# MLP activations at another offset in SBUF, and products that read and write their columns in short runs from two halves

## The chip, the cores and the metric

The kernel runs on one core of one Trainium2 chip. The metric is the device time of one execution in microseconds (us). TensorE (PE in the profile) does the matrix products, VectorE (DVE) and ScalarE (ACT) the element-wise work, GpSimd (POOL) some of it too; weights come from HBM by DMAs that the queue of SyncE (SP) issues.

## The reference, cut to what matters

A trunk of two layers over 512 tokens with 1024 channels, in float32. Each layer is a mixer and a gated MLP, both with a residual add. The MLP, which the change touches in both layers:

```python
def conv_ffn(x, w_up, conv_w, conv_b, w_down):
    hdn = causal_dwconv(x @ w_up, conv_w, conv_b)
    return (jax.nn.silu(hdn[..., :D_FF]) * hdn[..., D_FF:]) @ w_down
...
h = rmsnorm(x, norm_ffn[i]); x = x + conv_ffn(h, f_w_up[i], ...)      # D_FF = 2816, kernel of 3 taps
```

The mixer of layer 0 (an mLSTM) has an output gate, `h * jax.nn.sigmoid(o)` with `o` a slice of `x @ w_in`, 1024 columns wide; its product is the second place that the change touches.

## The kernel before, in words

Everything is held transposed: channels on the 128 partitions, the 512 tokens along the free axis. A float32 operand is split into a high and a low float32r part, and a product is three matrix products (`mm3`, L160 to L163): stationary high part times moving high part (L161), high times low (L162), low times high (L163). In all the products that the change touches the weights (`wh`, `wl`) are the stationary operand, 128 rows by 128 columns, and the activations are the moving one, 128 rows by 512 columns. Each of the three is one instruction that loads the weights (LDWEIGHTS) and one that streams the columns (MATMUL) and adds them to one bank of PSUM.

`proj` (L404) multiplies one unit of weights (8 blocks of 128x128) by the normed input `xh`, `xl`: 8 x 3 = 24 products into one bank. It makes the queries and keys (`qk_conv`), the output gates (`o_block`, L432, eight blocks), the up-projections of both MLPs (`ffn`, L593) and the input of the convolution module (`glu`).

`ffn` runs in two parts. Up: 22 times (`j`), two calls of `proj` into two banks `pa` and `pb`, then on VectorE and ScalarE the row factor of the norm, three taps, silu and the gate, which leave `yh[:, j, :]` and `yl[:, j, :]`, the two parts of the hidden activations. Down: for each of 8 output blocks `m`, 22 x 3 = 66 products of the down-weights by `yh` and `yl` into one bank. In the last MLP the last block (`m` = 7) is made in two halves of 256 columns, 132 products in all. So the first MLP has 44 x 24 = 1056 products up and 528 down, the second 1056 up, 462 down and those 132 halves, and the eight output gates are 192 products.

The units of weights come in a fixed order (`seq`). `next_unit` has up to four units in flight by DMA and splits two ahead, ScalarE the high part (L149), VectorE the low one (L150). The order of the instructions on each engine is laid down when the program is built, by a scheduler.

Where tiles lie in a partition of SBUF follows from the order and sizes of the pools. In the built program, byte addresses modulo 256 are: `xh` and `xl` 64, all eight pairs; each 128-column block of `wh` and `wl` 64; `yh` and `yl` 0 for every `j`, in both MLPs (`fp`, the pool of the MLP, starts with them). In the two projections after the mixers (`out_proj`, L576 to L580) the moving operand lies elsewhere: `gh` and `gl` of layer 0 start at 0, 32, 64, 96, 128, 160, 192 and 224, one pair of blocks each, `zht` and `zlt` of layer 1 at 128.

Of the kernel before, what the change touches and what calls it, by code (L numbers as in the profile page):

```python
# [9 lines left out]
F32 = mybir.dt.float32  # L10
# [4 lines left out]
P = 128  # L15
T = 512
D = 1024
KD = D // P
# [6 lines left out]
EPS = 1e-6  # L25
QSCALE = 128.0 ** -0.5
NEG = -1.0e30
NPH = 4                    # token phases of the convolution on the tensor engine
NTAU = T // NPH
NJ = (CK + 2 * NPH - 3) // NPH  # L30
GR = 68                    # rows: input gates at 0, running maximum at 32, forget gates at 64

# column offsets in the packed per-channel parameter array
_COLS = {}
_off = 0
for _n, _w in [("norm_mix", 16), ("norm_ffn", 16), ("norm_final", 8), ("mconv_w", 32),
# [9 lines left out]
def hybrid_trunk(ctx, tc, x_in, par_in, tph_in, wg_in, wv_in, wqk_in, wo_in, mout_in, cin_in,  # L46
# [20 lines left out]
    def small():  # L67
        return psms.tile([P, T], F32, tag="ms", name=nm("ms"))

# [1 line left out]
    par = const.tile([P, NPAR], F32, name="par")  # L71
    nc.scalar.dma_start(out=par[:, :16], in_=par_in[:, :16])

# [18 lines left out]
    G.memset(mhalf, -0.5)  # L92

    def warm(n, after=None):
        """Products that nobody reads, to keep the clock of the tensor engine up over a wait."""
        ps = bank()
        for _ in range(n):
            with tc.issue_after(after.ins) if after is not None else nullcontext():
                after = PE.matmul(ps[:, :P], ones, ones, start=True, stop=True)  # L99

# [1 line left out]
    seq = []  # L102
    for h in range(2):
        for u in range(4):
# [57 lines left out]
        PE.matmul(ps, lh, rl, start=False, stop=False)  # L162
        PE.matmul(ps, ll, rh, start=False, stop=stop)  # L163

# [1 line left out]
    xh = [None] * KD  # L166
    xl = [None] * KD

# [27 lines left out]
        return t[:, c].rearrange("p (a b) -> p a b", b=P)  # L196

    def to_rows(src, c, tag):
        """Values along the free axis, equal on all partitions -> [128 tokens, blocks]."""
        nb = (c.stop - c.start) // P  # L200
        dg = work.tile([P, T], F32, tag="tmp", name=nm("dg"), bufs=4)
        V.tensor_tensor(out=blocks(dg, c), in0=src,
                        in1=ident[:].unsqueeze(1).to_broadcast([P, nb, P]), op=ALU.mult)
        r4 = work.tile([P, NTB], F32, tag=tag, name=nm(tag))
        V.tensor_reduce(out=r4[:, :nb], in_=blocks(dg, c), op=ALU.add, axis=mybir.AxisListType.X)
        return r4

    def from_rows(r4, nb, pb):
        """[128 tokens, blocks] -> the values along the free axis on all partitions (PSUM)."""
        hl = work.tile([P, 2, NTB], F32R, tag="hl", name=nm("hl"))  # L210
        V.tensor_copy(hl[:, 0, :nb], r4[:, :nb])
        V.tensor_tensor(out=hl[:, 1, :nb], in0=r4[:, :nb], in1=hl[:, 0, :nb], op=ALU.subtract)
        for i in range(2):
            dg = work.tile([P, NTB, P], F32R, tag="tmp", name=nm("dgr"), bufs=4)
            v = V.tensor_tensor(out=dg[:, :nb], in0=ident[:].unsqueeze(1).to_broadcast([P, nb, P]),
                            in1=hl[:, i, :nb].bitcast(F32).unsqueeze(2).to_broadcast([P, nb, P]),
                            op=ALU.mult)
            p = PE.matmul(pb, onesr, dg[:, :nb].rearrange("p a b -> p (a b)"), start=i == 0, stop=i == 1)  # L218
        return v, p

    def col_mean(ps, t, c, w):
        """Sum over the partitions of t times the constant in w, on all partitions."""
        h = work.tile([P, T], F32R, tag="tmp", name=nm("ch"), bufs=4)
        l = work.tile([P, T], F32R, tag="tmp", name=nm("cl"), bufs=4)
        A.copy(h[:, c], t[:, c])
        V.tensor_tensor(out=l[:, c], in0=t[:, c], in1=h[:, c], op=ALU.subtract)
        PE.matmul(ps, w, h[:, c], start=True, stop=False)
        PE.matmul(ps, w, l[:, c], start=False, stop=True)
# [4 lines left out]
        return o4  # L233

    def row_sums(ps, t, c, w, start, stop):
        """Adds the sums over the partitions of t, times w, to ps: [128 tokens, 2 * blocks]."""
        nb = (c.stop - c.start) // P
        for b in range(nb):
            s = slice(c.start + b * P, c.start + (b + 1) * P)
            PE.matmul(ps[:, 2 * b : 2 * b + 2], t[:, s], w[:, :2], start=start and b == 0,  # L240
                      stop=stop and b == nb - 1)

    def norm_rows(nrm, c):
        """1 / rms of the tokens in c, [128 tokens, blocks]."""
        n = c.stop - c.start
        ps = small()
        col_mean(ps[:, :n], nrm.acc, c, invdr)
        r4 = to_rows(ps[:, :n].rearrange("p (a b) -> p a b", b=P), c, "ms4")
        V.tensor_scalar(out=r4[:, : n // P], in0=r4[:, : n // P], scalar1=EPS, scalar2=None,
                        op0=ALU.add)  # L250
        return rsqrt4(r4, n // P, "rs4")

    # the row factors of a norm are worked out between the first products of the next stage
    hooks = []

    def run_hook():
# [15 lines left out]

    rs = {}

    # ================= layer 0: mLSTM =================
    warm(9)
    nrm = Norm()
    first = wraw.tile([P, 1024], F32, tag="wr", name="wr0")
# [76 lines left out]

    pv = v_pair(0)

    # gates, channel-major: input gates on partitions 0-3, forget gates on 32-35
    wgh, wgl = next_unit()
    pg = small()  # L360
    for k in range(KD):
# [39 lines left out]
                                       in1=t[:, s:], op0=ALU.mult, op1=ALU.add)  # L401
        return v

    def proj(units, ps):  # L404
        wh, wl = units
        for k in range(KD):
            c = slice(k * P, (k + 1) * P)
            mm3(ps, wh[:, c], wl[:, c], xh[k], xl[k], k == 0, k == KD - 1)
            if k == 5:
                run_hook()  # L410

# [19 lines left out]

    def o_block(m, ahead=2):  # L432
        ps = bank()
        proj(next_unit(ahead), ps)
        sig[m] = mp.tile([P, T], F32, tag="sig", name=nm("sig"), bufs=4)
        V.tensor_tensor(out=sig[m], in0=ps, in1=rs["b"], op=ALU.mult)
        A.activation(sig[m], sig[m], AF.Sigmoid)
# [1 line left out]
    T0 = [0, 128, 256, 256]  # L439

    def att_decay(h):
        """exp of the decay from s to t less the running maximum; s on partitions, t free."""
        plf, pm = small(), small()
        for p, i in ((plf, h), (pm, NH + h)):
            PE.matmul(p, sel[:, i, :], sth, start=True, stop=False)
# [82 lines left out]
    q = qk(0)  # L528
# [60 lines left out]
    out_proj(gh, gl_, None, lambda m: ("norm_ffn", m))  # L589
    mctx.close()  # L590

    # ================= gated MLP with a depthwise convolution =================
    def ffn(l, g=None, last=False):  # L593
        fctx = ExitStack()
        fp = fctx.enter_context(tc.tile_pool(name=nm("ffn"), bufs=1))
        yh = fp.tile([P, NF, T], F32R, name=nm("yh"))
        yl = fp.tile([P, NF, T], F32R, name=nm("yl"))
        for j in range(NF):
            pa, pb = bank(), bank()
            proj(next_unit(), pa)  # L600
            proj(next_unit(), pb)
            ta = fp.tile([P, T], F32, tag="ta", name=nm("ta"), bufs=2)
            tb = fp.tile([P, T], F32, tag="tb", name=nm("tb"), bufs=2)
            both = ((pa, ta, l * 44 + j), (pb, tb, l * 44 + NF + j))
# [85 lines left out]

    ffn(0, lambda m: ("norm_mix", 8 + m))

    # ================= layer 1: convolution module =================
    cctx = ExitStack()
    cp = cctx.enter_context(tc.tile_pool(name="conv", bufs=1))
    DVE_CH, POOL_CH, PE_CH = (0, 2, 4), (1,), (3, 5, 6, 7)
# [4 lines left out]
    pdvr = cp.tile([P, P], F32R, name="pdvr")  # L701
    A.copy(pdvr, p128)
    cacc = {c: cp.tile([P, T], F32, name=f"cacc{c}") for c in range(8)}
    # 1 where the partition lies in the block of NPH partitions
    tph = cp.tile([P, 8 * 4 * NJ * NPH], F32, name="tph")
    nc.sync.dma_start(out=tph, in_=tph_in)
    msk4 = cp.tile([P, P // NPH, 1], F32, name="msk4")
# [74 lines left out]
                o = 32 * (2 * hf + g)  # L782
                (nc.scalar if g == 0 else nc.sync).dma_start(out=back[o : o + 32], in_=co[:, g])

    # taps for the vector engine and GpSimd, handed out between the products
    vtaps, gtaps = [], []

    def background(nv, ng):
# [9 lines left out]
    FIRST, LAST = PE_CH[0], PE_CH[-1]  # L798

    def shift():  # L800
        """The mean of one block of channels, by which all values are shifted before their sums."""
        d[FIRST] = cp.tile([P, T], F32, name=f"d{FIRST}")
        A.activation(d[FIRST].rearrange("p (t q) -> p t q", q=NPH),
                     cacc[FIRST].rearrange("p (q t) -> p t q", q=NPH), AF.Identity,
                     bias=pcol("dw_b", FIRST))
        pk = small()
        col_mean(pk, d[FIRST], slice(0, T), pdvr)
        A.copy(kb, pk)
        V.tensor_tensor(out=d[FIRST], in0=d[FIRST], in1=kb, op=ALU.subtract)
        G.tensor_copy(s1, d[FIRST])  # L810
        A.activation(s2, d[FIRST], AF.Square)
# [49 lines left out]
    sq4 = stats(4, V)  # L861
    sq7 = stats(LAST, None)

    # layer norm over channels
    pr1, pr2, pmu = small(), small(), bank()
    for i, (t1, t2) in enumerate(((s1, s2), (d[LAST], sq7))):
        row_sums(pr1, t1, slice(0, T), invd, i == 0, i == 1)
# [34 lines left out]
def _layout(inputs):  # L902
    f = {k: np.asarray(v) for k, v in inputs.items()}

    def ch(a):  # [..., C] -> [128, ... * C/128], channel c = m * 128 + p
        a = a.reshape(a.shape[:-1] + (-1, P))
        return np.moveaxis(a, -1, 0).reshape(P, -1)

    def taps(w):  # [K, C] -> [128, C/128 * K]
        k, c = w.shape  # L910
        return w.reshape(k, c // P, P).transpose(2, 1, 0).reshape(P, -1)

    def cols(w, n=P):  # [K, N] -> [N/n, 128, K/128 * n]
        k, c = w.shape
        return w.reshape(k // P, P, c // n, n).transpose(2, 1, 0, 3).reshape(c // n, P, -1)

    # gate biases: input gates on partitions 0-3, forget gates on 32-35
    bg = np.zeros((P, 1), np.float32)
    bg[0:4, 0], bg[32:36, 0] = f["m_b_gates"][0][:4], f["m_b_gates"][0][4:]
    # taps by token phase: dph[c * NPH + p, m, g, j, q] = w[K - 1 - (NPH * j + q - p), m * 128 + g * 32 + c]  # L920
    dw = f["c_dw_w"][0].reshape(CK, KD, 4, P // 4)
    dph = np.zeros((P // NPH, NPH, KD, 4, NJ, NPH), np.float32)
    for p in range(NPH):
# [50 lines left out]
```

## Time and profile before

| what | value |
|---|---|
| two timed runs | 1192.22 and 1192.62 us, median 1192.42 |
| profiled execution, first to last instruction (span) | 1191.0 us |
| that lies outside the span, median less span | 1.4 us |
| PE busy | 1134.3 us, 95% of the span |
| PE in the chain that ended last | 84% |

The profiled execution is known by its span alone, so it stands beside the median with what lies around the span. Matrix products are pipelined: the time shown for one (0.39 us) is longer than the distance from its start to the start of the next, and that distance, called pace here, is what a stage of back-to-back products costs. It is read from the starts in a timeline: last start less first start, divided by the products between.

### The profile page before, as it was taken

The numbers are of one execution on the slowest core, as the hardware profiler recorded it, in microseconds if no ns is written. First come the engines' busy times: TensorE is split into PE (matmuls) and PEld (weight loads), VectorE is DVE, ScalarE is ACT, GpSimd is POOL, SyncE is SP. The second block draws the span as 40 slices with busy tenths as digits, with TensorE's granted clock in tenths as the row PEclk, the third lists the DMA queues.
The fourth block names the chain that finished last, engine by engine and source line by source line (L and its number), as shares of the span: only waits on it lengthen the run. The fifth ranks groups of instructions, "written<-read, shape, count | busy, mean of one in ns | idle before, by whom it ended". The sixth has DMA issues, their size and how long they took to land.

```text
span 1191.0 us, 13476 instructions
## 1 busy us (share of the span) xinstructions
PE 1134.3 (95%) x5226; PEld 939.7 (79%) x5226; DVE 788.6 (66%) x1022; ACT 510.8 (43%) x713; POOL 174.8 (15%) x126
## 2 busy tenths in 40 slices
PE   9999999999999999999998757699999999999996
PEld 7788888888888888888887647588888888888886
DVE  6788875487777775332479999874877777752222
ACT  6556774354444443222244522363544444432221
POOL 4000001100000000000267857021000000000002
PEclk9999999999999999999998879699999999999998
DMA  6222123223232323233332112022232323233322
GB/s 247 89 89 71 54 74 103 90 89 106 89 106 89 105 86 92 90 97 98 110 105 62 62 44 67 14 88 89 92 103 90 106 89 106 84 98 89 93 62 71
DMA packets 36369, 106.85 MB, mean 90 GB/s; under 512 B 4049, under 2 KB 10321, under 8 KB 36305
## 3 DMA queue, kind: packets, MB, share of 16 engines
q1 hardware_dynamic: 31728, 103.25, 27.2%
q10 hardware_dynamic: 4576, 2.74, 0.8%
q8 instruction: 41, 0.67, 0.2%
q14 instruction: 24, 0.19, 0.0%
HBM read 101.78 MB, written 2.10 MB: 87 GB/s over the span
## 4 chain that ended last, share of the span: by engine, by line
PE 84%; DVE 13%; issue 1%; ACT 1%; DMA 1%; POOL 0%; ACTq 0%; POOLq 0%; SPq 0%; DVEq 0%
PE mm L161 25%; PE mm L162 25%; PE mm L163 25%; DVE cacc L744 8%; PE mm L580 2%; PE mm L577 2%; PE mm L576 2%; DVE wl L150 2%; PE ms L240 1%; PE mm L99 0%; DMA xall<-in_dram 0%; PE ms L218 0%; DVE u L722 0%; DVE se L453 0%; DVE s L826 0%
## 5 line engine op out<-in xcount | busy, mean ns | idle before, releaser
L163 PE MATMUL mm<-xh,wl 128*128 128x512 f32 x960 | 375.6, 391 | 3.3 <-DVE wl L150 3.3
L161 PE MATMUL mm<-xh,wh 128*128 128x512 f32 x960 | 375.6, 392 | 0.0
L162 PE MATMUL mm<-xl,wh 128*128 128x512 f32 x960 | 375.4, 391 | 0.0
L150 DVE TENSOR_TENSOR wl<-wr,wh 128x1024 fp32r<-128x1024 f32 (+1 forms) x192 | 236.5, 1235 | 165.5 <-ACT wh L149 163.3
L149 ACT CAST wh<-wr 128x1024 fp32r<-128x1024 f32 (+1 forms) x192 | 197.4, 1030 | 296.1 <-PE mm L162 243.6
L163 PEld LDWEIGHTS mm<-xh,wl 128*128 128x128 f32 x960 | 181.4, 189 | 41.9 <-DVE wl L150 3.7
L162 PEld LDWEIGHTS mm<-xl,wh 128*128 128x128 f32 x960 | 181.4, 189 | 37.9
L161 PEld LDWEIGHTS mm<-xh,wh 128*128 128x128 f32 x960 | 181.5, 189 | 37.2
L193 POOL TENSOR_TENSOR acc<-acc,sq 128x512 f32<-128x512 f32 x30 | 43.3, 1444 | 746.7 <-ACT sq L191 746.2
L161 PE MATMUL mm<-yh,wh 128*128 128x512 f32 (+1 forms) x374 | 142.3, 380 | 0.0
L162 PE MATMUL mm<-yl,wh 128*128 128x512 f32 (+1 forms) x374 | 142.3, 380 | 0.0
L163 PE MATMUL mm<-yh,wl 128*128 128x512 f32 (+1 forms) x374 | 142.2, 380 | 0.0
L606 DVE TENSOR_TENSOR mm<-mm,rsb 128x512 f32<-128x512 f32 x88 | 60.8, 695 | 76.0 <-PE mm L163 73.1
L744 DVE SCALAR_TENSOR_TENSOR cacc<-u,par,cacc 128x501 f32<-128x501 f32 (+27 forms) x80 | 102.1, 1321 | 0.1
L161 PEld LDWEIGHTS mm<-yh,wh 128*128 128x128 f32 x374 | 70.0, 187 | 15.5
L162 PEld LDWEIGHTS mm<-yl,wh 128*128 128x128 f32 x374 | 70.0, 187 | 15.3
L163 PEld LDWEIGHTS mm<-yh,wl 128*128 128x128 f32 x374 | 70.0, 187 | 15.2
L616 ACT CAST yh<-ta 128x512 fp32r<-128x512 f32 x44 | 27.3, 620 | 104.6 <-DVE ta L615 104.6
L611 DVE SCALAR_TENSOR_TENSOR ta<-mm,par,ta 128x511 f32<-128x511 f32 x88 | 65.6, 745 | 1.3
L611 DVE SCALAR_TENSOR_TENSOR tb<-mm,par,tb 128x511 f32<-128x511 f32 x88 | 65.5, 746 | 1.4
L614 ACT ACTIVATE ta<-ta 128x512 f32<-128x512 f32 x44 | 27.8, 632 | 79.4 <-DVE ta L611 79.4
L741 POOL TENSOR_TENSOR cacc<-cacc,cprod 128x511 f32<-128x511 f32 (+29 forms) x30 | 49.5, 1651 | 24.1 <-ACT cprod L739 22.4
(237 smaller groups left out, 1200.5 us busy)
## 6 DMA issues: line engine op xcount, KB each, us to landing
wr<-in_dram SPq DMA_DIRECT2D x175, 512.0 KB, 3.5
wr<-in_dram SPq DMA_DIRECT2D x16, 384.0 KB, 3.1
xall<-in_dram SPq DMA_DIRECT2D x8, 256.0 KB, 6.4
us<-u ACTq DMA_DIRECT2D x16, 64.0 KB, 2.1
out_dram<-xall SPq DMA_DIRECT2D x2, 384.0 KB, 3.5
tph<-in_dram SPq DMA_DIRECT2D x1, 576.0 KB, 4.5
wr<-in_dram SPq DMA_DIRECT2D x2, 256.0 KB, 3.9
cacc<-co ACTq DMA_DIRECT2D x8, 64.0 KB, 2.4
```

The costliest lines, as they stand in the source:

```text
L149: st["last"] = A.copy(hi[:, :n], r[:, :n])
L150: V.tensor_tensor(out=lo[:, :n], in0=r[:, :n], in1=hi[:, :n], op=ALU.subtract)
L161: PE.matmul(ps, lh, rh, start=start, stop=False)
L162: PE.matmul(ps, lh, rl, start=False, stop=False)
L163: PE.matmul(ps, ll, rh, start=False, stop=stop)
L193: e.tensor_tensor(out=nrm.acc[:, c], in0=nrm.acc[:, c], in1=sq[:, c], op=ALU.add)
L606: V.tensor_tensor(out=ps, in0=ps, in1=rs["b"], op=ALU.mult)
L611: V.scalar_tensor_tensor(out=t[:, s:], in0=ps[:, : T - s], scalar=pcol("fconv_w", m * 3 + 2 - s), in1=t[:, s:], op0=ALU.mult, op1=ALU.add)
L614: A.activation(ta, ta, AF.Silu)
L616: A.copy(yh[:, j, :], ta)
L741: G.tensor_tensor(out=a[:, s:], in0=a[:, s:], in1=p[:, s:], op=ALU.add)
L744: V.scalar_tensor_tensor(out=cacc[j][:, s:], in0=u[:, : T - s], scalar=dw(j, CK - 1 - s), in1=cacc[j][:, s:], op0=ALU.mult, op1=ALU.add)
```

## The change

There are two edits. (1) Each MLP takes a small unused tile at the head of its pool, 16 floats (64 bytes) in the first MLP and 8 floats (32 bytes) in the second. All tiles of that pool move up by as much: `yh` and `yl` lie at 64 modulo 256 in the first MLP and at 32 in the second, and `ta` and `tb` move with them. (2) `proj` takes a run length `e`. With `e` above 0 the moving operand and the PSUM output are seen as two halves of 256 columns that are cut in runs of `e` columns, and the product walks them as run 0 of the first half, run 0 of the second, run 1 of the first, and so on. Input and output are walked alike, so each column lands where it did. The output gates use `e` = 4 (128 runs of 16 bytes), the up-projection of the first MLP `e` = 32 (16 runs of 128 bytes), and all other calls `e` = 0, which is the plain operand of before. Comments go too.

```diff
-    def proj(units, ps):
+    def runs(t, e):
+
+        return t.rearrange("p (h c e) -> p c h e", h=2, e=e) if e else t
+
+    def proj(units, ps, e=0):
         wh, wl = units
         for k in range(KD):
             c = slice(k * P, (k + 1) * P)
-            mm3(ps, wh[:, c], wl[:, c], xh[k], xl[k], k == 0, k == KD - 1)
+            mm3(runs(ps, e), wh[:, c], wl[:, c], runs(xh[k], e), runs(xl[k], e), k == 0, k == KD - 1)
...
     def o_block(m, ahead=2):
         ps = bank()
-        proj(next_unit(ahead), ps)
+        proj(next_unit(ahead), ps, 4)
...
         fp = fctx.enter_context(tc.tile_pool(name=nm("ffn"), bufs=1))
+        fp.tile([P, 16 >> l], F32, name=nm("pad"))
         yh = fp.tile([P, NF, T], F32R, name=nm("yh"))
         yl = fp.tile([P, NF, T], F32R, name=nm("yl"))
         for j in range(NF):
             pa, pb = bank(), bank()
-            proj(next_unit(), pa)
-            proj(next_unit(), pb)
+            proj(next_unit(), pa, 32 if l == 0 else 0)
+            proj(next_unit(), pb, 32 if l == 0 else 0)
```

No engine's instructions change their order; the shapes of the touched products do. On PE, where the second key block ends and the first output gate begins (`mm_640` and `mm_688` are their banks), before:

```order
L162 MATMUL mm_640<-xl_17_162,wh_605 128x512
L163 MATMUL mm_640<-xh_16_161,wl_606 128x512
L161 MATMUL mm_688<-xh_2_110,wh_643 128x512
L162 MATMUL mm_688<-xl_3_111,wh_643 128x512
L163 MATMUL mm_688<-xh_2_110,wl_644 128x512
L161 MATMUL mm_688<-xh_4_116,wh_643 128x512
```

and now:

```order
L162 MATMUL mm_640<-xl_17_162,wh_605 128x512
L163 MATMUL mm_640<-xh_16_161,wl_606 128x512
L161 MATMUL mm_688<-xh_2_110,wh_643 128x64x2x4
L162 MATMUL mm_688<-xl_3_111,wh_643 128x64x2x4
L163 MATMUL mm_688<-xh_2_110,wl_644 128x64x2x4
L161 MATMUL mm_688<-xh_4_116,wh_643 128x64x2x4
```

The 192 products of the gates are walked as 64 x 2 runs of 4 columns. On PE, where the first MLP goes from the first block of its up-projection to the next (`mm_2059`, then `mm_2160`), now:

```order
L161 MATMUL mm_2059<-xh_256_2044,wh_2062 128x8x2x32
L162 MATMUL mm_2059<-xl_257_2045,wh_2062 128x8x2x32
L163 MATMUL mm_2059<-xh_256_2044,wl_2063 128x8x2x32
L161 MATMUL mm_2160<-xh_229_1803,wh_2106 128x8x2x32
L162 MATMUL mm_2160<-xl_230_1804,wh_2106 128x8x2x32
```

Its 1056 products are 8 x 2 runs of 32 columns, in the places where 128x512 stood.

## Rows read from the trace of the kernel before

**Rows 1.** The page: busy times, the clock in 40 slices, the chain by engine.

```profile
PE 1134.3 (95%) x5226; PEld 939.7 (79%) x5226; DVE 788.6 (66%) x1022; ACT 510.8 (43%) x713; POOL 174.8 (15%) x126
...
PEclk9999999999999999999998879699999999999998
...
PE 84%; DVE 13%; issue 1%; ACT 1%; DMA 1%; POOL 0%; ACTq 0%; POOLq 0%; SPq 0%; DVEq 0%
```

**Rows 2.** Busy time by stretch: start:end, length, busy us (instructions), granted clock, DMA share.

```profile
core 0: us, PE busy (x) PEld busy (x) DVE busy (x) ACT busy (x) POOL busy (x), PEclk, DMA share, GB/s
58.00:175.00 117.00, 116.07 (x591) 98.51 (x590) 97.56 (x185) 80.95 (x150) 4.04 (x4) 1.00 0.22 75
...
220.40:460.70 240.30, 240.30 (x1061) 198.93 (x1060) 175.63 (x226) 106.99 (x134) 1.02 (x1) 1.00 0.30 96
460.70:583.90 123.20, 123.20 (x529) 98.75 (x529) 39.90 (x43) 33.58 (x40) 7.77 (x6) 1.00 0.31 93
...
815.30:1055.60 240.30, 240.30 (x1061) 198.95 (x1060) 175.69 (x226) 105.69 (x133) 1.02 (x1) 1.00 0.30 96
1055.60:1172.00 116.40, 116.40 (x539) 94.96 (x538) 33.20 (x35) 32.60 (x39) 7.71 (x6) 1.00 0.26 75
```

**Rows 3.** Timeline, PE, first up-projection: start, time shown; 45 products apart.

```profile
329.74 0.39 PE L162 MATMUL mm<-xl,wh 128*128 128x512 f32 x1
...
339.94 0.39 PE L162 MATMUL mm<-xl,wh 128*128 128x512 f32 x1
```

**Rows 4.** Timeline, PE, first down-projection; 27 products apart.

```profile
479.66 0.39 PE L161 MATMUL mm<-yh,wh 128*128 128x512 f32 x1
...
485.96 0.39 PE L161 MATMUL mm<-yh,wh 128*128 128x512 f32 x1
```

**Rows 5.** Timeline, PE, output gates of layer 0; 12 products apart.

```profile
69.77 0.39 PE L161 MATMUL mm<-xh,wh 128*128 128x512 f32 x1
...
72.49 0.39 PE L161 MATMUL mm<-xh,wh 128*128 128x512 f32 x1
```

**Rows 6.** Chain that ended last, projections after the mixers: start, us, eight products.

```profile
190.79 1.87 PE mm L580 x8
...
797.15 1.83 PE mm L580 x8
```

**Rows 7.** Timeline, PE, projection after the mLSTM: moving operands at mixed offsets.

```profile
192.72 0.39 PE L577 MATMUL mm<-gl,wh 128*128 128x512 f32 x1
192.96 0.40 PE L576 MATMUL mm<-gh,wh 128*128 128x512 f32 x1
```

**Rows 8.** Timeline, PE, last block in halves of 256 columns; 18 products apart.

```profile
1174.95 0.28 PE L161 MATMUL mm<-yh,wh 128*128 128x256 f32 x1
...
1176.99 0.28 PE L161 MATMUL mm<-yh,wh 128*128 128x256 f32 x1
```

**Rows 9.** Groups of the first up-projection: busy us, mean ns, idle before.

```profile
L162 PEld LDWEIGHTS mm<-xl,wh 128*128 128x128 f32 x352 | 66.1, 188 | 13.9
...
L150 DVE TENSOR_TENSOR wl<-wr,wh 128x1024 fp32r<-128x1024 f32 x44 | 53.9, 1224 | 11.6 <-ACT wh L149 10.7
...
L606 DVE TENSOR_TENSOR mm<-mm,rsb 128x512 f32<-128x512 f32 x43 | 29.7, 695 | 36.1 <-PE mm L163 34.6 <-ACT rsb L269 1.5
```

## The prediction, made before the changed kernel ran

> **What bounds the kernel now.** I read the page first: PE is busy 95% of the span and 84% of the chain that ended last [rows 1]. Then the stretches: both MLPs are PE from end to end, 240.3 of 240.3 us and 123.2 of 123.2 us, at the full granted clock, while VectorE is busy 175.6 of 240.3 us at most; the stretch of the mLSTM with the output gates is PE too, 116.1 of 117.0 us [rows 2]. Next to nobody is waited for there, so what sets their length is the pace of the products, and the timeline gives it. Up, at 64 modulo 256 for moving operand and weights: (339.94 - 329.74) / 45 = 226.7 ns [rows 3]. The output gates, with the same operands: 2.72 / 12 = 226.7 ns [rows 5]. Down, with `yh` at 0 and the weights at 64: 6.30 / 27 = 233.3 ns [rows 4]. Shape, clock and order of instructions are the same in both, and VectorE is less busy in the slower one (39.9 of 123.2 us) [rows 2], so neither the clock nor another engine's traffic makes the difference; what is left is where the operands lie. Pace times count gives the stages back: 1056 x 226.7 = 239.4 us of the 240.3, 528 x 233.3 = 123.2 us. The projections after the mixers bear it out: 1.87 / 8 = 234 ns with the moving operand at mixed offsets, 1.83 / 8 = 229 ns with it at 128 [rows 6]. [...]
>
> **First MLP down (528 products).** `yh` and `yl` come to 64, the offset at which `xh` is read against the same weights. I take the pace of the up-projection: 528 x (226.7 - 233.3) = -3.5 us. The bounds: 226.7 is the lowest pace in any row, so -3.5 on one side; on the other the longest distance in the mixed stage, 192.96 - 192.72 = 240 ns [rows 7], which is 528 x 6.7 = +3.5 us.
>
> [...]
>
> **Second MLP down (462 products, 132 halves).** At 32 the operand lies halfway between two offsets that have rows (0 and 64). No row shows 32 alone; the stage with all offsets mixed has 234 ns. Bounds: 226.7 and 240 ns, which are -3.1 and +3.1 us. I take the middle of the two neighbours, 230 ns: 462 x (230 - 233.3) = -1.5 us. [...]
>
> **Up-projection and gates in runs (1056 and 192 products).** [...] The nearest row is that of the halves: two products of 256 columns cost 226.6 ns together, no more than one of 512 and less than the one of the same operands, 233.3, so beginning anew in the middle cost nothing there. I take 0 for both. [...]
>
> [...]
>
> **The sum.** -3.5 - 1.5 + 0 + 0 = -5.0 us. The profiled span of 1191.0 us becomes 1186.0, and with the 1.4 us outside it that the median of 1192.42 shows, 1187.4 us. Everything behind these stages starts earlier by what they save: the convolution module in between waits for VectorE's taps, which follow the products of its own input, so it moves as a whole.
>
> **Rivals.** [...] (b) *Each break costs.* The product pauses when it jumps to the other half, in reading SBUF or in writing PSUM. A product makes 15 jumps at `e` = 32 and 127 at `e` = 4: 1056 x 15 + 192 x 127 = 40,224. From 5.0 us / 40,224 = 0.12 ns per jump it eats the gain. [...] For it: nothing has shown such a stream at speed. Against it: the halves [rows 8]. (c) *The offset does nothing and the runs neither*: the difference between up and down comes from something that I don't see, and the time stays at 1192.4 us.
>
> **How the numbers follow.** Forecast 0.33, with its own range 1184 to 1192 us (the bounds of the second MLP, and some of the first). (a) 0.27, 1171 to 1183. (b) 0.32: half of that under 24 us, half above, since four cycles per jump are as conceivable as one. (c) 0.08. The range leaves out the far end of (a) and the far half of (b): 1175 to 1216 us. A measurement of this kernel can tell about 2% from no change, 23.8 us: slower by that is the far half of (b), 0.15; faster by that would be below 1168.6 us, past even the whole of (a), 0.02; within, 0.83.
>
> **What would show it.** In the changed profile: the first down-projection at 226.7 ns per product, 119.7 us long instead of 123.2 (right), or still 233.3 (the address is not the cause). The second: its pace tells what 32 is worth. [...] I am wrong if the up-projection of the first MLP differs from the second by more than 3 us.

## The result, and the profile of the changed kernel

Two timed runs took 1204.07 and 1205.78 us, median 1204.92, against 1192.42 before: a ratio of 1.0104 with the interval [1.0075, 1.0133]. The kernel became about 12.5 us slower, where 5 us less was forecast. The profiled span grew from 1191.0 to 1202.4 us, by 11.4 us.

The page of the changed kernel, its busy times and the granted clock, answers to [rows 1]; the third line is the group of all products of `xh` and `wl` that `proj` makes, the plain ones included (busy us, mean ns, idle before):

```profile
PE 1144.4 (95%) x5226; PEld 940.9 (78%) x5226; DVE 791.3 (66%) x1022; ACT 510.7 (42%) x713; POOL 174.8 (15%) x126
...
PEclk9999999999999999999999969699999999999998
...
L163 PE MATMUL mm<-xh,wl 128*128 128x512 f32 x960 | 380.5, 396 | 3.3 <-DVE wl L150 3.3
```

The same group before:

```profile
L163 PE MATMUL mm<-xh,wl 128*128 128x512 f32 x960 | 375.6, 391 | 3.3 <-DVE wl L150 3.3
```

PE makes the same 5226 products in 10.1 us more, at the same clock (mean granted 0.976, before 0.974), and stands idle for 3.3 us in all ahead of the 960 products of that group, as before. So nothing new is waited for: the products themselves take longer. Which ones, the stretches tell (start:end, length, busy us per engine, clock; answers to [rows 2]):

```profile
core 0: us, PE busy (x) PEld busy (x) DVE busy (x) ACT busy (x) POOL busy (x), PEclk, DMA share, GB/s
224.40:475.20 250.80, 250.80 (x1062) 200.43 (x1061) 177.30 (x226) 105.82 (x134) 1.02 (x1) 1.00 0.29 92
475.20:594.80 119.60, 119.60 (x530) 98.99 (x529) 39.94 (x43) 33.71 (x40) 7.87 (x6) 1.00 0.32 95
826.20:1066.60 240.40, 240.40 (x1062) 199.07 (x1061) 175.67 (x226) 105.75 (x133) 1.02 (x1) 1.00 0.30 96
```

Compared with [rows 2] the first up-projection starts 4.0 us later (224.40 for 220.40) and lasts 250.8 us for 240.3, the first down-projection 119.6 for 123.2, the convolution module 231.4 for 231.4, the second up-projection 240.4 for 240.3, and what follows to the end 135.8 for 135.4: 4.0 + 10.5 - 3.6 + 0.1 + 0.4 = 11.4 us, the whole of it. In the stage that grew, the clock is 1.00, VectorE is busy 177 of 251 us, and the loading of weights 200 of 251.

The paces, from the timeline of PE of the changed kernel. In order of time: gates, first up, first down, second down, halves; they answer to [rows 5], [rows 3], [rows 4] and [rows 8], and the second down-projection to [rows 4] too:

```profile
69.16 0.41 PE L161 MATMUL mm<-xh,wh 128*128 128x512 f32 x1
...
72.17 0.42 PE L161 MATMUL mm<-xh,wh 128*128 128x512 f32 x1
...
332.84 0.40 PE L162 MATMUL mm<-xl,wh 128*128 128x512 f32 x1
...
343.49 0.40 PE L162 MATMUL mm<-xl,wh 128*128 128x512 f32 x1
...
489.61 0.39 PE L161 MATMUL mm<-yh,wh 128*128 128x512 f32 x1
...
495.73 0.39 PE L161 MATMUL mm<-yh,wh 128*128 128x512 f32 x1
...
1070.19 0.40 PE L161 MATMUL mm<-yh,wh 128*128 128x512 f32 x1
...
1076.49 0.40 PE L161 MATMUL mm<-yh,wh 128*128 128x512 f32 x1
...
1186.37 0.28 PE L161 MATMUL mm<-yh,wh 128*128 128x256 f32 x1
...
1188.50 0.28 PE L161 MATMUL mm<-yh,wh 128*128 128x256 f32 x1
```

The gates: 3.01 us / 12 products = 250.8 ns, where it was 226.7. First up: 10.65 / 45 = 236.7, where it was 226.7. First down: 6.12 / 27 = 226.7, where it was 233.3. Second down: 6.30 / 27 = 233.3, unchanged. Halves: 2.13 / 18 = 118.3, where it was 113.3. Note that the time shown beside a start (0.39 or 0.40 us) says next to nothing of this: only the distance of the starts does.

So the runs cost 1056 x 10 = 10.6 us and 192 x 24 = 4.6 us, the new address brought 528 x 6.6 = 3.5 us in the first MLP, and in the second it cost 132 x 5 = 0.7 us in the halves: 12.4 us in sum, beside 12.5 between the medians and 11.4 between the two spans. Per jump the two costs are 10 / 15 = 0.67 ns at runs of 32 columns and 24 / 127 = 0.19 ns at runs of 4: no fixed price per jump.

### The profile page after: what moved, and what is told of

The parts are those of the page before. It is cut to its first block, busy times and chain, and to the rows that moved or that the text cites. A ratio compares the mean times of both kernels' runs of the same rounds, so it can differ in the third digit from the quotient of the medians.

```text
span 1202.4 us, 13474 instructions
## 1 busy us (share of the span) xinstructions
PE 1144.4 (95%) x5226; PEld 940.9 (78%) x5226; DVE 791.3 (66%) x1022; ACT 510.7 (42%) x713; POOL 174.8 (15%) x126
## 4 chain that ended last, share of the span: by engine, by line
PE 84%; DVE 13%; issue 1%; ACT 1%; DMA 1%; POOL 0%; ACTq 0%; POOLq 0%; SPq 0%; DVEq 0%
PE mm L162 25%; PE mm L161 25%; PE mm L163 25%; DVE cacc L749 8%; PE mm L584 2%; PE mm L581 2%; PE mm L580 2%; DVE wl L150 2%; PE ms L240 1%; DMA xall<-in_dram 0%; PE ms L218 0%; DVE u L727 0%; DVE se L457 0%; DVE s L831 0%; PE mm L521 0%
## 5 line engine op out<-in xcount | busy, mean ns | idle before, releaser
L163 PE MATMUL mm<-xh,wl 128*128 128x512 f32 x960 | 380.5, 396 | 3.3 <-DVE wl L150 3.3
L161 PE MATMUL mm<-xh,wh 128*128 128x512 f32 x960 | 380.8, 397 | 0.0
L162 PE MATMUL mm<-xl,wh 128*128 128x512 f32 x960 | 380.5, 396 | 0.0
```

The lines of the kernel that those rows point to most:

```text
L161: PE.matmul(ps, lh, rh, start=start, stop=False)
```

## The experiments

Below, a pace is the mean distance between the starts of successive products of one stage, waits left out; the timelines show two starts each, so a pace worked out from them can differ by some tenths of a ns from that of the whole stage. "Offset" is the byte address of the moving operand less that of the weights, modulo 256. Where one time is given, the kernel was run once, beside kernels before at 1192.8 to 1194.7 us; what is read from it rests on paces, which repeat between runs (runs of 32 take 236.7 ns in the changed kernel and in `sides`, a plain product at the offset 192 takes 233.3 in the kernel before and in `weights_shift`), and not on the total. Several kernels add other columns than the reference does, or leave out part of the sums; the expectations say which.

Two theories were in the field for most of it. Theory M: the stream of columns meets the stream that loads the next weights in one part of SBUF, and the offset and the runs change how often. Theory S: the stream of columns stands in its own way, by the order in which it comes back to the same bytes modulo 256.

### Each edit alone

```diff
# pads_only
+        if (16, 8)[l]:
+            fp.tile([P, (16, 8)[l]], F32, name=nm("pad"))
# runs_only
+    def proj(units, ps, rd=0, wr=0):
+            mm3(runs(ps, wr), wh[:, c], wl[:, c], runs(xh[k], rd), runs(xl[k], rd), k == 0, k == KD - 1)
...
+        proj(next_unit(ahead), ps, 4, 4)
...
+            proj(next_unit(), pa, *((32, 32), (0, 0))[l])
```

> Edit 1 alone: yh and yl at 64 modulo 256 in the first MLP, at 32 in the second, no runs. If the two edits add up (theory: each stage's pace depends on its own operands alone), the first down-projection runs at 226.7 ns per product, the second at 233.3, its halves at 118 to 120 ns, both up-projections and the gates at 226.7: 1192.4 - 3.5 + 0.8 = 1189.7 us. Rival: part of the gain in the first down-projection came from the runs ahead of it, and the time is 1192 or more.

> Edit 2 alone. If the edits add up: gates at 250 ns per product, first up-projection at 236.6, both down-projections at 233.3 as before; span 1191.0 + 192 x 23.4 + 1056 x 9.9 = 1191.0 + 4.5 + 10.5 = 1206 us. Rival: the new place of ta and tb or of yh had a part in the slower up-projection, which then runs below 236 ns here.

The pads alone took 1189.77 us (1189.28 to 1191.80) beside 1193.73, a ratio of 0.9973 [0.9964, 0.9983]: 3.2 us less by the ratio (the medians are 4.0 apart). First down 226.7 ns, second down 233.3, halves 118.2, gates and up 226.7 to 227. The runs alone took 1207.45 us: gates 250.3, first up 236.7, both down-projections 233.3. The paces of the two edits appear unchanged in the changed kernel, so they don't act on each other, and the runs hold the whole loss.

### Reading or writing in runs

```diff
# sides: proj(units, ps, rd, wr); queries and keys written in runs, gates read in runs
+        proj(next_unit(), ps, 0, 4)
...
+        proj(next_unit(ahead), ps, 4, 0)
...
+            proj(next_unit(), pa, *((32, 0), (0, 32))[l])
```

> The two sides of a run apart: the columns of the products named are left in another order in PSUM, so what follows works on other tokens. Read in runs, written plainly: gates with 4 columns, first up-projection with 32. Read plainly, written in runs: queries and keys with 4 columns, second up-projection with 32. Theory R (the order in which SBUF is read costs): gates 250 ns and first up-projection 236.6 as in the changed kernel, queries, keys and second up-projection 226.7. Theory W (the order in which PSUM is written costs): the other way round, 226.7 for the first two and 250 and 236.6 for the other two. Theory J (the jump itself costs, on whichever side): all four between 226.7 and the values of the changed kernel.

Timeline of PE: the gates and the first up-projection, which read in runs, then the second up-projection, which writes in runs of 32:

```profile
70.73 0.41 PE L161 MATMUL mm<-xh,wh 128*128 128x512 f32 x1
...
74.50 0.41 PE L161 MATMUL mm<-xh,wh 128*128 128x512 f32 x1
...
332.76 0.40 PE L161 MATMUL mm<-xh,wh 128*128 128x512 f32 x1
...
344.83 0.40 PE L161 MATMUL mm<-xh,wh 128*128 128x512 f32 x1
...
935.03 0.39 PE L161 MATMUL mm<-xh,wh 128*128 128x512 f32 x1
...
946.59 0.39 PE L161 MATMUL mm<-xh,wh 128*128 128x512 f32 x1
```

Read in runs: 3.77 us / 15 products = 251 ns and 12.07 / 51 = 236.7. Written in runs: 11.56 / 51 = 226.7, the plain pace; the queries and keys, written in runs of 4, are at 227 to 228 ns. All of the cost is in reading SBUF, none in writing PSUM: outputs in runs of 4 and of 32 floats cost nothing here.

### How long a run must be

The lengths were 8 for queries and keys, 16 for the gates, 64 in the first up-projection and 128 in the second.

```diff
+        proj(next_unit(), ps, 8, 8)
...
+        proj(next_unit(ahead), ps, 16, 16)
...
+            proj(next_unit(), pa, *((64, 64), (128, 128))[l])
```

> Runs of other lengths, read and written alike: queries and keys 8 columns (63 jumps), gates 16 (31 jumps), first up-projection 64 (7 jumps), second 128 (3 jumps). Theory J (a price per jump): the pace over 226.7 ns falls with the jumps; with 0.66 ns per jump from the runs of 32 the four stages run at 268, 247, 231 and 229 ns, with 0.18 ns from the runs of 4 at 238, 232, 228 and 227. Theory R (the stream meets the weights' stream according to where it is, not how often it jumps): no such order; the pace can be as high at 64 or 128 columns as at 32, 235 ns or so, and nothing runs below 226.7.

Timeline of PE, the gates with runs of 16 and the first up-projection with runs of 64:

```profile
71.23 0.40 PE L161 MATMUL mm<-xh,wh 128*128 128x512 f32 x1
...
74.83 0.40 PE L161 MATMUL mm<-xh,wh 128*128 128x512 f32 x1
...
333.09 0.39 PE L161 MATMUL mm<-xh,wh 128*128 128x512 f32 x1
...
344.65 0.39 PE L161 MATMUL mm<-xh,wh 128*128 128x512 f32 x1
```

| run, columns (bytes) | 4 (16) | 8 (32) | 16 (64) | 32 (128) | 64 (256) | 128 (512) |
|---|---|---|---|---|---|---|
| pace, ns | 250.3 | 243.3 | 240.0 | 236.7 | 226.7 | 226.7 |
| above the plain pace, ns | 23.6 | 16.6 | 13.3 | 10 | 0 | 0 |

The first two lines give 3.60 / 15 = 240.0 ns, the others 11.56 / 51 = 226.7. Neither theory of this run foresaw both the slow short runs and the free long ones. There is an edge between 128 and 256 bytes: seven jumps per product cost nothing, fifteen cost 10 ns. The two halves of a row are 1024 bytes apart, four times 256. With runs of 256 bytes the walk through the addresses modulo 256 is then that of a plain stream; with shorter runs every part of the 256 bytes comes twice in short order.

### Is it the address against the weights, or the order of the walk?

First the place of the weights. One unused tile at the head of their pool puts them at 128; `xh` and `xl` stay at 64, while `yh` and `yl`, which have no pads here, move with the weights from 0 to 64.

```diff
+    wraw.tile([P, 16], F32, tag="pad", name="wpad", bufs=1)
```

> The kernel before with the weights 64 bytes further on (wh and wl at 128 modulo 256, and yh and yl at 64 with them; xh and xl stay at 64). Theory M (what counts is where the moving stream is against the weights' stream: the two meet): xh lies 64 bytes behind the weights, as yh did and does, so queries, keys, gates and both up-projections go from 226.7 to 233.3 ns and the down-projections stay at 233.3; span 1191.0 + (384 + 2112) x 6.7 = 1208 us or a little more. Rival A (the moving operand's own address counts): up-projections stay at 226.7 and the down-projections, now at 64, come to 226.7: 1191.0 - 990 x 6.7 ns = 1184 us.

Timeline of PE, first up-projection, plain:

```profile
332.65 0.40 PE L162 MATMUL mm<-xh,wh 128*128 128x512 f32 x1
...
344.55 0.39 PE L162 MATMUL mm<-xh,wh 128*128 128x512 f32 x1
```

1212.44 us: the plain up-projections went from 226.7 to 11.90 / 51 = 233.3 ns. There the moving operand did not move, so its own address can't be the cause: where it lies against the weights counts. The down-projections stay at 233.3, at 192 from the weights as before, though `yh` itself moved. The projection after the second mixer has the same offset, 64, in this kernel as in the one before, and goes at 233.0 ns here and at 229 there; so the offset alone doesn't fix the pace either.

Then jumps that keep the walk in phase. `parity` reads the down-projections in runs of 32 with 15 jumps, in the first MLP from rows 544 floats apart (2176 bytes, 128 more than a multiple of 256), in the second from rows 512 apart.

```diff
+    def jump(y, k, l):
+        f = y.rearrange("p n t -> p (n t)")
+        if l == 0:
+            k = min(k, NF - 3)
+            f = f[:, k * T : k * T + 1088].rearrange("p (h x) -> p h x", x=544)[:, :, :512]
+            return f.rearrange("p h (i s) -> p i h s", s=64)[:, :, :, :32]
+        k = min(k, NF - 2)
+        f = f[:, k * T : k * T + 1024].rearrange("p (h x) -> p h x", x=512)[:, :, :256]
+        return f.rearrange("p h (i s) -> p i h s", s=32)
...
-                    mm3(ps, wh[:, c], wl[:, c], yh[:, k, :], yl[:, k, :], k == 0, k == NF - 1)
+                    mm3(ps, wh[:, c], wl[:, c], jump(yh, k, l), jump(yl, k, l), k == 0, k == NF - 1)
```

> yh and yl at 64 in both MLPs, and the down-projections read 16 runs of 32 columns with 15 jumps each; they read columns of the next block of channels for part of their own, so the sums are of other columns. First MLP: each jump goes 128 bytes on modulo 256 (runs at 0, 17, 2, 19, ... times 128 bytes), so modulo 256 the stream walks as a plain one. Second MLP: jumps by a multiple of 256 (runs at 0, 16, 1, 17, ...), so each half of 256 bytes is walked twice before the next, as in the changed kernel. Theory M: 226.7 ns in the first, 236.6 in the second. Theory J (the jumps cost): the same in both, 236.6 ns.

Timeline of PE, first and second down-projection:

```profile
479.99 0.39 PE L161 MATMUL mm<-yh,wh 128*128 128x512 f32 x1
...
491.55 0.39 PE L161 MATMUL mm<-yh,wh 128*128 128x512 f32 x1
...
1070.08 0.40 PE L161 MATMUL mm<-yh,wh 128*128 128x512 f32 x1
...
1081.44 0.40 PE L161 MATMUL mm<-yh,wh 128*128 128x512 f32 x1
```

The same shape, the same number of jumps, the same length of run: 11.56 / 51 = 226.7 ns in phase, 11.36 / 48 = 236.7 ns with each part of the 256 bytes read twice. `jumps_in_phase` drives it further, with 31 jumps and runs of 16 in the first MLP and 127 jumps and runs of 4 in the second, both in phase (rows 528 and 516 floats apart):

```diff
+        e = (16, 4)[l]
+        f = y.rearrange("p n t -> p (n t)")[:, k * T : k * T + 2 * (T + e)]
+        f = f.rearrange("p (h x) -> p h x", x=T + e)[:, :, :T]
+        return f.rearrange("p h (i s) -> p i h s", s=2 * e)[:, :, :, :e]
```

> yh and yl at 64 in both MLPs; the down-projections read runs of 16 columns (31 jumps) in the first MLP and of 4 columns (127 jumps) in the second, with jumps that go one run on modulo 256 bytes, so that modulo 256 the walk is that of a plain stream; part of the columns read are those of the next blocks, so the sums are of other columns. Theory S (the stream stalls on its own order modulo 256) and theory M (its place against the weights' stream): 226.7 ns in both. Theory J (short runs or jumps cost by themselves): 240 and 250 ns, as the runs of 16 and of 4 by turns.

Timeline of PE, first and second down-projection:

```profile
480.11 0.39 PE L161 MATMUL mm<-yh,wh 128*128 128x512 f32 x1
...
491.67 0.39 PE L161 MATMUL mm<-yh,wh 128*128 128x512 f32 x1
...
1070.04 0.39 PE L161 MATMUL mm<-yh,wh 128*128 128x512 f32 x1
...
1081.60 0.39 PE L161 MATMUL mm<-yh,wh 128*128 128x512 f32 x1
```

11.56 / 51 = 226.7 ns in both, with 127 jumps as with none; the run took 1188.24 us. A short run and a jump are free in themselves, down to runs of 16 bytes. What costs is which bytes modulo 256 follow on which: 226.7 ns in phase, 236.7 and 250.3 by turns, with runs of 32 and of 4. That 256 is the measure is read from the lengths: runs of 128 bytes from halves 1024 bytes apart are a plain walk modulo 128 and cost 10 ns; runs of 256 bytes come twice modulo 512 and cost nothing. A run of 16 bytes costs 24 ns in the gates and nothing here, so its length alone does not decide it.

`repeats` keeps runs of 32 (rows 528 and 544 floats apart, 256 columns from each) and varies the order alone.

```diff
+        x = T + (16, 32)[l]
+        f = y.rearrange("p n t -> p (n t)")[:, k * T : k * T + 2 * x]
+        f = f.rearrange("p (h x) -> p h x", x=x)[:, :, :256]
+        return f.rearrange("p h (i s) -> p i h s", s=32)
```

> yh and yl at 64; down-projections in runs of 32 columns by turns from two places 64 bytes apart modulo 256 in the first MLP, 128 bytes apart in the second (other columns in the sums again). In units of 64 bytes modulo 256 the walks are 0 1 1 2 2 3 3 0 ... and 0 1 2 3 2 3 0 1 ..., where the changed kernel has 0 1 0 1 2 3 2 3 and a plain stream 0 1 2 3. Theory S: a unit that is read again at once costs most, so the first is slower than 236.7 ns; the second comes back less often than the changed kernel and lies between 226.7 and 236.7. Theory J: 236.7 in both.

Timeline of PE, first and second down-projection:

```profile
479.68 0.41 PE L161 MATMUL mm<-yh,wh 128*128 128x512 f32 x1
...
491.92 0.41 PE L161 MATMUL mm<-yh,wh 128*128 128x512 f32 x1
...
1069.83 0.39 PE L161 MATMUL mm<-yh,wh 128*128 128x512 f32 x1
...
1081.73 0.39 PE L161 MATMUL mm<-yh,wh 128*128 128x512 f32 x1
```

12.24 / 51 = 240.0 ns and 11.90 / 51 = 233.3 ns. In units of 64 bytes modulo 256 the walks so far are:

| walk | 0 1 2 3 0 1 2 3 | 0 1 2 3 2 3 0 1 | 0 1 0 1 2 3 2 3 | 0 1 1 2 2 3 3 0 | 0 0 1 1 2 2 3 3 |
|---|---|---|---|---|---|
| from | plain | repeats, second | first up, runs of 32 | repeats, first | gates, runs of 16 |
| ns | 226.7 | 233.3 | 236.7 | 240.0 | 240.0 |

So at one length of run and one number of jumps the order alone moves the pace, from 226.7 to 240.0 ns, and the walks that read a unit twice at once are the slowest. That is in favour of theory S, but a plain rule, the sooner back the slower, does not follow. Carried on, `repeats` in the second MLP walks 0 1 2 3 2 3 0 1 0 1 2 3, which is the walk of the first up-projection begun one run later: a unit comes back after 2 and 6 by turns in both, not less often as the expectation says. Yet the paces, both of the second down-projection, are 233.3 ns in `repeats` and 236.7 in `parity`. The first MLP of `repeats` and the gates with runs of 16 are such a pair too, and have one pace, 240.0 ns. Where in the product the repeats fall can matter, then; what the rule is stays open.

### What theory M would still need

If runs cost because they meet the weights, another offset should change their price. In the plainest form of M the stream by turns and that of the weights go through the 256 bytes at one speed, so that their distance stays what it was at the start. Two kernels read the down-projections by turns from the halves, the first MLP and the second at the offsets 128 and 64 in one kernel, 192 and 128 in the other:

```diff
# turns_128_64, then turns_192_four
+            fp.tile([P, (48, 32)[l]], F32, name=nm("pad"))
+                    mm3(runs(ps, (32, 32)[l]), wh[:, c], wl[:, c], runs(yh[:, k, :], (32, 32)[l]), ...)
...
+            fp.tile([P, (0, 48)[l]], F32, name=nm("pad"))
+                    mm3(runs(ps, (32, 4)[l]), wh[:, c], wl[:, c], runs(yh[:, k, :], (32, 4)[l]), ...)
```

> Down-projections in runs of 32 columns by turns from both halves, read and written alike, with yh and yl 128 bytes (first MLP) and 64 bytes (second MLP) ahead of the weights modulo 256. [...] Rival (runs by turns cost 10 ns at any offset, or the two streams have other speeds): 233 to 240 ns in both.

> As the run before, with other values: first MLP runs of 32 columns with yh and yl 192 bytes ahead (64 behind), second MLP runs of 4 columns with 128 bytes ahead. Theory M in its plainest form: the runs of 4, which stay half the period away from the weights' stream all along, go below 226.7 ns where the gates with 0 had 250; the runs of 32 at 192 lie between those at 128 and at 0. Rival: 250 ns for the runs of 4 at any offset.

Timeline of PE, runs of 32 at the offset 128 (`turns_128_64`, first down-projection), then runs of 4 at 128 (`turns_192_four`, second):

```profile
479.67 0.40 PE L161 MATMUL mm<-yh,wh 128*128 128x512 f32 x1
...
491.74 0.40 PE L161 MATMUL mm<-yh,wh 128*128 128x512 f32 x1
```

```profile
1080.02 0.42 PE L161 MATMUL mm<-yh,wh 128*128 128x512 f32 x1
...
1091.27 0.41 PE L161 MATMUL mm<-yh,wh 128*128 128x512 f32 x1
```

At the offset 128 runs of 32 take 12.07 / 51 = 236.7 ns, at 64 and at 192 they take 236.7 too, and runs of 4 at 128 take 11.25 / 45 = 250.0. At offset 0 it was 236.7 and 250.3. Where the weights lie did not change the pace of a stream in runs. What the runs cost over a plain stream at the same offset does: 10 ns at 0, but 3.4 at 128 and at 192, where the plain stream takes 233.3 (the table of offsets below). The two costs don't add up.

The last trial of M loads fewer weights beside the same stream: 64 or 32 of 128 weight columns in six of the eight blocks of each unit. What tells the theories apart is the difference between runs and plain, 10 ns for runs of 32 and 23.6 for runs of 4 with all 128 columns.

```diff
+            n = P if k in (0, KD - 1) else 64
+            c = slice(k * P, k * P + n)
+            mm3(runs(ps[:n], wr), wh[:, c], wl[:, c], runs(xh[k], rd), runs(xl[k], rd), k == 0, k == KD - 1)
```

> The runs of the changed kernel (gates 4 columns, first up-projection 32, second plain), but in these products the blocks 1 to 6 of each unit use 64 of their 128 weight columns, so half of the output channels lack their sums. [...] Theory S: the differences stay 10 and 23 ns.

> As the run before with 32 of the 128 weight columns. [...]

Timeline of PE with 32 columns, first up-projection (runs) and second (plain):

```profile
332.63 0.40 PE L161 MATMUL mm<-xh,wh 128*32 128x512 f32 x1
...
344.65 0.40 PE L161 MATMUL mm<-xh,wh 128*32 128x512 f32 x1
...
935.29 0.39 PE L161 MATMUL mm<-xh,wh 128*32 128x512 f32 x1
...
946.35 0.39 PE L161 MATMUL mm<-xh,wh 128*32 128x512 f32 x1
```

With 128, 64 and 32 weight columns the runs of 32 take 236.7, 234.4 and 235.8 ns, the runs of 4 take 250.3, 247.9 and 247.8, and the plain products 226.7, 229.2 and 230.6. The difference between runs of 32 and plain falls from 10 to 5.2 and 5.2 ns. By S it stays 10 in both, by M, in which only half and a quarter of the weights are there to be met, it falls to 5 and 2.5; but by M the plain products become faster too, and they became slower (with 32 columns their starts are 220 to 240 ns apart in the timeline, with 128 columns 220 to 230). So this pair bears out neither theory: the number of weight columns changes both paces, in a way that neither describes. It also shows that the plain pace at offset 0 does not fall with the number of weight columns loaded: 226.7, 229.2 and 230.6 ns.

### The price of the offset for plain products

Pads of 24 and 32, 48 and 56, and 40 and 0 floats put `yh` at other offsets.

```diff
+        if (24, 32)[l]:                      # then (48, 56), then (40, 0)
+            fp.tile([P, (24, 32)[l]], F32, name=nm("pad"))
```

> The kernel before with yh and yl 32 bytes (first MLP) and 64 bytes (second MLP) ahead of the weights modulo 256. Theory M: 64 gives 229 ns as the projection after the convolution, whose operands lie so; 32 lies between that and 226.7. Rival (the offset counts modulo 128, or 64 bytes are one unit): 64 ahead gives 233.3, as 64 behind.

> The kernel before with yh and yl 128 bytes (first MLP) and 160 bytes (second MLP) ahead of the weights modulo 256. Theory M with a period of 256 bytes: neither need equal the stage at 0; the mixed stage after the mLSTM, which has all offsets, says some 232 to 235 ns. Rival (period 128): 128 ahead gives 226.7 as 0 does.

> The kernel before with yh and yl of the first MLP 96 bytes ahead of the weights modulo 256; the second MLP as before. It is the one multiple of 32 that has no run yet. Theory M, from its neighbours at 64 (229) and 128 (233.7): 229 to 234 ns; the second stays at 233.3.

The three took 1192.84, 1195.06 and 1192.88 us. With the weights at 64, the plain pace by offset is:

| offset | 0 | 32 | 64 | 96 | 128 | 160 | 192 | 224 |
|---|---|---|---|---|---|---|---|---|
| pace, ns | 226.7 | 233.3 | 229.0 | 233.4 | 233.3 | 234.3 | 233.3 | 233.3 |

One offset is good, one is not far from it, all others cost 6.6 to 7.6 ns. The pace at 32 is not between its neighbours, as was expected of it. (192 is the kernel before, 224 the second MLP of the changed one.)

### A kernel with the offset 0 where it fits

No runs; `yh` at 64 in both MLPs, and `gh`, `zht` and `zlt` of the two `out_proj` stages put at 64 as well; `gl` keeps its mixed offsets.

```diff
+    mp.tile([P, 16], F32, name="vpad")
+    vh = [mp.tile([P, 1088], F32R, tag=f"vgh{h}", name=f"vh{h}")[:, : NTB * VW].rearrange("p (a b) -> p a b", b=VW) for h in range(NH)]
...
+            fp.tile([P, (16, 16)[l]], F32, name=nm("pad"))
...
+    cp.tile([P, 48], F32, name="cpad")
```

> No runs; the offset of the up-projections (moving operand and weights alike modulo 256) given to all else that can have it: yh, yl at 64 in both MLPs, zht and zlt at 64, gh at 64 (gl does not fit and stays mixed). Theory M: both down-projections 226.7 ns (-3.5 and -3.1 us), the projection after the convolution 226.7 instead of 229 (-0.5), that after the mLSTM partly (-0.5), the halves of the last block 121 instead of 115 (+0.8): 1192.4 - 6.8 = 1185.6 us. Rival: the second down-projection keeps 233 ns whatever its offset, and the time is 1189.

1188.12 us (1185.51 to 1188.22) beside 1192.77, a ratio of 0.9948 [0.9934, 0.9961]: 6.2 us less by the ratio (the medians are 4.7 apart), the lowest median of all. Both down-projections stand at 226.7 ns, the projection after the second mixer at 227.2 instead of 229, that after the first at 230.8 instead of 232.4. The median is 2.5 us above the 1185.6 expected. The halves, at 120 ns instead of 113.3, were in that sum. In the profiled execution the output gates begin at 66.22 us, where they began at 64.30 before: 1.9 us of the 2.5 arise ahead of the gates. The kernel of `offsets_32_64`, whose edit leaves the mixers alone, begins them at 65.97, so this is not the price of the offsets.

## Why the prediction was wrong, step by step

- **First MLP down, -3.5 us**: right, to the tenth. 226.7 ns where `yh` lies at the offset of `xh`, 119.6 us for the stage. Moving an address by 64 bytes changed the pace by 6.6 ns. That PE waits for another engine there, no run shows: it is busy 119.60 of the 119.60 us.
- **Second MLP down, -1.5 us**: wrong in size; it is 0. The middle between the paces at 0 and 64 supposed a slope, and there is none: 32 bytes off (the offset 224) costs the same 233 ns as 64 off.
- **Halves**, for which the sum has no term: they went from 113.3 to 118.3 ns, +0.7 us.
- **Runs, "I take 0 for both"**: this is the step that failed. It cost 10.6 and 4.6 us. The value came from the nearest row, the halves: beginning anew in the middle cost nothing, so a break was held to be free. The row was true and did not say it. The second half starts 1024 bytes after the first, so its walk goes on in phase, and so do runs of 256 bytes, which are free as well. The runs of 16 and 128 bytes in the change come back to the same bytes modulo 256 at once. The row was a lucky one, too: the halves were read at the offset 192, and at the offset 0, that of `xh`, two halves take 2 x 120 = 240 ns where one product of 512 takes 226.7.
- **Rival (b), each break costs**: right in sign, but its mechanism is not the cause. With a price per jump the gates, with 127 jumps for 15, would have grown by eight times as much per product as the first up-projection; they grew by 24 ns, that by 10. No price per jump fits 0.67 and 0.19 ns, and 127 jumps in phase cost nothing.
- **Rival (a)**, 1171 to 1183 us: wrong in sign, the runs made the products slower. The meeting with the weights, in its plain form, is not borne out either: runs of 32 keep 236.7 ns at four offsets. **Rival (c)**: wrong in both parts, the address counts (6.6 ns) and the runs cost (10 and 24 ns).
- **The range**, 1175 to 1216 us, held the time, and the change is within 2%, as was given 0.83; the forecast itself was on the wrong side. The sign set for being wrong came: the first up-projection took 250.8 us, the second 240.4, 10.4 us apart where 3 were allowed. The shorter products that the 1171 to 1183 us of (a) need, and the cycles per jump by which the chance of (b) is halved, no run shows: the lowest pace of a product of 512 columns was 226.7 ns, and a jump cost 0.67 ns in the runs of 32 by turns, 0.19 in those of 4 and nothing in phase.

What stays open: what inside SBUF makes the order modulo 256 count, which no run shows; why the same walk begun one run later takes 233.3 ns and not 236.7, and why fewer weight columns narrow the difference between runs and plain; why the offset against the weights counts for plain products and not for runs; and why the difference alone does not fix it, as the shifted weights showed.

## What to carry to other kernels

Where PE is busy from end to end, read the pace from the starts in the timeline, stage by stage, and compare stages of one shape: 6.6 and 10 ns per product were the whole difference in the MLPs here. In this kernel a plain moving operand of 512 columns was fastest at the same address modulo 256 as the weights, both at 64; no other common address was tried, and the difference alone does not fix the pace, so try it and measure. If an operand is read in pieces, let the pieces continue each other modulo 256 bytes, as pieces of 256 bytes at multiples of 256 do (226.7 ns, the plain pace). Before a row is taken as the price of something new, ask what the two have in common and what not: here the length of a run and its phase were different things, and one row held both.

## What was not expected of the hardware

- The order in which a product reads SBUF counts modulo 256 bytes: 226.7 ns in plain order, up to 250.3 in runs of 16 bytes by turns, with the same bytes read; 127 jumps in phase cost nothing.
- Writing PSUM in runs of 16 or 128 bytes costs nothing (227 to 228 and 226.7 ns).
- The same stream beside fewer weight columns is not faster: 226.7 ns with 128, 229.2 with 64, 230.6 with 32.
- The best place for a product of 512 columns is not the best for one of 256: halves go at 113.3 ns at the offset 192, at 118.3 at 224 and at 120 at 0, where products of 512 are fastest.
